# Duration table and operand margin of the clock that orders the matmuls, in a hybrid attention, gMLP and RWKV-7 layer

## The chip, the cores and the metric

The kernel runs on one core of a Trainium2 chip. The metric is the device time of one execution in microseconds (us). Five engines work side by side, each through its own instructions in program order: TensorE (PE in the profile, with its weight loads as PEld), VectorE (DVE), ScalarE (ACT), GpSimd (POOL) and SyncE (SP), which here issues almost all DMAs. An engine waits for another through semaphores. What stands early in an engine's program and is not ready holds back all that stands behind it on that engine.

## The reference

One layer with 2048 frames and 1024 channels, in float32. All branches read one projection of the normalised input, are gated, projected and merged:

```python
h = rmsnorm(x, pre_g[l]) * (1 + scale[:, None]) + shift[:, None]
q_lat, kv_lat, k_rope, gm_in, rw_in, z, g_logit = split_last(h @ w_in[l], IN_SPLITS)
y_mla = mla_mixer(...)      # 8 heads, softmax over chunk-causal keys
y_gm = gmlp_mixer(...)      # spatial gating inside blocks of 128 frames
y_rw, v_first = rwkv7_mixer(...)   # recurrence over all frames, a 64x64 state per head
branches = branches * jax.nn.silu(z)...
proj = jnp.einsum('bsnw,nwd->bsnd', branches, w_br[l])
merged = jnp.sum(proj * jax.nn.sigmoid(g_logit)..., axis=2)
x = x + gate[:, None] * rmsnorm(merged @ w_out[l], post_g[l])
```

## The kernel before

The sequence is cut into four blocks of 512 frames (`NSB` = 4). After a first stage that prepares block 0, each block s goes through two stages. `wkv(s)` is the RWKV branch: for four pairs of heads `project` and `prepare` make operands, `inverses` solves small triangular systems on VectorE in 31 dependent steps, `advance` makes the per-chunk matrices and `states` walks the eight chunks of the block one after the other (matmul `pss<-S,QG`, then two VectorE copies `S<-pss`, then the next chunk). `attention(s)` is the softmax branch: 8 heads with two units each; a unit computes scores (`pss<-kh,qh` and two more matmuls, since each float32 product is made of three matmuls on a high and a low part), takes minimum and exponential (`p`), transposes the result in groups of two key tiles (`pst<-consts,p`), splits it into `ph` (ScalarE copy) and `pw` (VectorE subtraction) and multiplies with the values (`pso<-ph,v`, `pso<-pw,v`). The last block ends with `finish`.

The large projections (`gemm`, matmuls into `pd`, 128x512 each, three per pair of operands) do not depend on these chains, and fill PE between their steps. Their weights come from DRAM, as raw weights that are split and stored the first time, and as stored parts (`kept`) afterwards.

No order of PE is written down. The program is generated by coroutines, and `Pace` keeps a clock while it is generated. Every emitted instruction passes through `Pace.note` (line 123 is the wrapper, which is why all profile rows say L123). `note` gives it a duration from small formulas by engine and size and places it in that engine's list of busy times, so each buffer has a time at which it is written or released. `Pace.run` then chooses which coroutine goes on: each yields the operands that it needs next, `ready` turns them into a time, and the one with the lowest time is stepped. Coroutines have ranks. The two chains of a stage (`behind`, `ahead`) and their helpers have ranks below 2. `todo` (rank 3, the next block's inputs) and `later` (rank 4, gates, branch projections, merges) hold the filler. Two rules tie filler to chains: a chain step that has to wait for an operand gets its time raised by `MARG` when it is compared, so filler that is ready is preferred unless the chain step is early by more than that; and in attention, filler is drawn as a share `SHARE[s]` of the chains' matmul time. The amount of filler in the whole program is fixed. The queue also supplies `backlog`, by which `split_lo` and `split` send the low part of new weights to VectorE or GpSimd.

The lines of the choice:

```python
r = k = self.ready(th)
if first and r > self.t:
    continue
if r > 0 and th[0] < 2:
    k += MARG
```

Of the kernel before, what the change touches and what calls it, by code (L numbers as in the profile page):

```python
# [36 lines left out]
DLAT = 0.8  # L37
EAR = 8.0
LAG = 1
MARG = 0.2  # L40
HOP = 0.25
SLOW = 1.0
KD = D // P
# [49 lines left out]
class Pace:  # L93
# [60 lines left out]
    def note(self, i):  # L154
        eng = str(i.engine).split(".")[-1]
        dma = "DMA" in type(i).__name__
        src, dst, n, full, f32 = [], [], 1, 0, False
        for l, aps in ((src, i.ins), (dst, i.outs)):
            for a in aps:
                ap = getattr(a, "bass_ap", None)  # L160
                if ap is None:
                    continue
                l.append(ap.tensor.name)
                m = 1
                for _, c in a.ap[1:]:
                    m *= c
                full += l is src and m > 1
                if dma:
                    m = 4 * m * a.ap[0][1]
                if eng != "PE" or l is dst:  # L170
                    n = max(n, m)
                elif a.dtype == F32:
                    f32 = True
        dep = 0.0
        for x in src:
            dep = max(dep, self.after(self.wrote.get(x), eng))
        for x in dst:
            for e in self.used.get(x, {}).items():
                dep = max(dep, self.after(e, eng))
        if eng == "PE":  # L180
            if f32 and not i.is_transpose:
                dur = 2 * max(.111, n * 2 / 2400)
            elif f32:
                dur = max(.108, n * 2 / 2400)
            else:
                dur = max(.061, n / 2400 + .0135)
            (r, c), (nr, nc) = i.tile_position, i.tile_size
            if dep <= self.t and all(r >= b or r + nr <= a for a, b in self.beside[1]):

                at = self.beside[0]  # L190
                self.beside[1].append((r, r + nr))
            else:
                at = max(self.t, dep)
                self.beside = at, [(r, r + nr)]
            t, p = max(self.t, at + dur), self.t
            self.pe += t - max(p, at)
            self.t = t
        elif dma:
            dur = n / 3.6e5
            t = self.slot("queue", max(dep, self.t - self.early), .45) + 1.1  # L200
            t = self.slot("DMA", t, dur) + dur + DLAT
            eng = "DMA"
        else:
            psum = any(x.startswith(("pd", "ps")) for x in src)
            op = type(i).__name__
            if eng == "Activation":
                f = str(i.func).split(".")[-1]
                if f in ("Exp", "Gelu", "Sin") and f != self.table or f == "Tanh" and self.table not in ("Exp", "Gelu"):
                    self.table = "Exp" if f == "Tanh" else f
                    t = self.slot(eng, max(dep, self.t - self.early), 1.28)  # L210
                dur = .08 + n * .00084 + .04 * (not psum) + .09 * (len(src) > 1) + .09 * (len(dst) > 1)
            elif eng == "DVE":
                dur = .065 + n / (960 if psum or full > 1 or n < 128 else 1920) + .065 * (full < len(src))
                if "Reciprocal" in op:
                    dur = .07 + n * .0063
                elif "Scan" in op or "Reduce" in op:
                    dur = n * (.0021 if "Scan" in op else .00118)
            else:
                dur = .12 + n * .00216 if n <= 512 else .55 + n * .0013
                if n <= 16 and "TensorTensor" in op:  # L220
                    dur = .3 + n * .165
            dur *= SLOW

            port = ("port",) if eng == "Pool" or eng == "DVE" and not psum else ()
            t = self.slot(eng, max(dep, self.t - self.early), dur, port) + dur
        for x in dst:
            self.wrote[x] = (eng, t)
        for x in src + dst:
            u = self.used.setdefault(x, {})
            u[eng] = max(u.get(eng, 0.0), t)  # L230
# [60 lines left out]
    def run(self, until, share=0.0, spare=lambda: True):  # L291
# [3 lines left out]
        while not until():  # L295
            best, key, at = None, self.INF, 0.0
            for first in ((3, 4, 0) if debt > 0 else (0,)):
                for th in self.threads:
# [5 lines left out]
                    if r > 0 and th[0] < 2:  # L304
                        k += MARG
                    if not first and th[0] == 4 and not spare():
# [1463 lines left out]
```

## Time and profile before

| | |
|---|---|
| time, median of 3 runs | 3148.54 us (3146.9 to 3155.53) |
| the profiled execution's own time | 3146.36 us |
| its span, first to last instruction | 3144.4 us |
| PE busy | 2927.0 us (93%) |
| DVE, ACT, POOL busy | 1731.6, 1216.7, 621.5 us |
| DMA | 654.17 MB, mean 208 GB/s |
| mean granted TensorE clock | 0.964 |

The span is one timeline of the core. An engine's busy share is an average over stages with different limits. The granted clock is the share of TensorE's full speed in a stretch: 1.0 is the higher of its two levels, 0.5 the lower, and a value between is a mix in time. A row of the view of windows gives, for one stretch, the busy time of each engine with the count of its instructions, the granted clock, the share of DMA engines in use and the rate. Stages lie at these times: first stage 0 to 236 us, `wkv(0)` 236 to 624, `attention(0)` from 624, then the stages of blocks 1 and 2, `wkv(3)` to 2712, `attention(3)` 2712 to 3027, `finish` to the end.

### The profile page before, as it was taken

Reading aid. Unit: us, or ns where it says so; the run is one execution under the profiler, and the core shown is the slowest. Engines: PE = TensorE matmul, PEld = TensorE weight load, DVE = VectorE, ACT = ScalarE, POOL = GpSimd, SP = SyncE. Lnnn points to the kernel's source line nnn. Section 1 sums busy time; section 2 is a strip of 40 time slices with the busy share of each in tenths; the row PEclk is TensorE's granted clock in tenths of the full one; section 3 lists DMA queues with packets and bytes.
Section 4 is the critical chain, followed back from the end, with each engine's and each line's share of the span. In section 5 each row is a group of like instructions: output and inputs, shape, how many; then the busy total and the mean of one; then the engine's idle time right before and its main releaser. Section 6 shows DMA issues by size and latency. Waiting matters only on the chain. (4 is left out here: it accounts for less than half of the span.)

```text
span 3144.4 us, 47954 instructions
## 1 busy us (share of the span) xinstructions
PE 2927.0 (93%) x16156; PEld 2391.6 (76%) x16156; DVE 1731.6 (55%) x4578; ACT 1216.7 (39%) x2806; POOL 621.5 (20%) x618
## 2 busy tenths in 40 slices
PE   5889998789999999999999998999999999999997
PEld 4667776668867787878877776887787777788876
DVE  6434767365366654466356664446645665566632
ACT  4324433353333424444232323544433232466621
POOL 2223232241022212122011101113201110222210
PEclk8999999879999999999999998999999999999998
DMA  8888855767566678765676577556558657744366
GB/s 273 271 271 264 251 182 182 242 210 229 200 210 223 192 226 265 225 196 166 211 251 199 166 230 231 185 177 209 155 169 250 198 171 230 224 137 128 113 207 204
DMA packets 524962, 654.17 MB, mean 208 GB/s; under 512 B 141648, under 2 KB 254380, under 8 KB 524716
## 3 DMA queue, kind: packets, MB, share of 16 engines
q1 hardware_dynamic: 524544, 651.06, 65.9%
q8 instruction: 128, 2.10, 0.3%
q14 instruction: 118, 0.97, 0.1%
q10 hardware_dynamic: 172, 0.05, 0.0%
HBM read 461.91 MB, written 189.01 MB: 207 GB/s over the span
## 5 line engine op out<-in xcount | busy, mean ns | idle before, releaser
L123 PE MATMUL pd<-hh,wh 128*128 128x512 f32 x1952 | 814.5, 417 | 19.3 <-ACT wh L123 10.3
L123 PE MATMUL pd<-hh,wl 128*128 128x512 f32 x1952 | 776.2, 398 | 6.1 <-DVE wl L123 4.3
L123 PE MATMUL pd<-hl,wh 128*128 128x512 f32 x1952 | 774.6, 397 | 2.5 <-DVE hl L123 1.5
L123 PEld LDWEIGHTS pd<-hh,wh 128*128 128x128 f32 x1952 | 374.5, 192 | 102.9 <-ACT wh L123 13.2
L123 PEld LDWEIGHTS pd<-hh,wl 128*128 128x128 f32 x1952 | 372.9, 191 | 94.7 <-DVE wl L123 8.3
L123 PEld LDWEIGHTS pd<-hl,wh 128*128 128x128 f32 x1952 | 374.8, 192 | 70.2 <-DVE hl L123 3.4
L123 DVE TENSOR_TENSOR pw<-pst,ph 128x512 fp32r<-128x512 f32 (+2 forms) x352 | 197.0, 568 | 255.2 <-ACT ph L123 253.6
L123 PE MATMUL pd<-brh,wh 128*128 128x512 f32 x576 | 252.0, 438 | 23.0 <-DVE gt L123 13.6
L123 ACT ACTIVATE ph<-pst 128x512 fp32r<-128x512 f32 (+2 forms) x352 | 171.7, 497 | 235.8 <-PE pst L123 197.8
L123 PE MATMUL pd<-brl,wh 128*128 128x512 f32 x576 | 232.4, 404 | 1.3 <-DVE brl L123 1.3
L123 PE MATMUL pd<-brh,wl 128*128 128x512 f32 x576 | 232.4, 403 | 0.0
L123 DVE TENSOR_SCALAR_CACHE_REDUCE p<-pss 128x512 f32<-128x512 f32 (+2 forms) x320 | 192.6, 607 | 62.6 <-PE pss L123 58.7
L123 ACT ACTIVATE p<-p,nm 128x512 f32<-128x512 f32 (+3 forms) x288 | 189.8, 661 | 79.1 <-DVE nm L123 78.9
L123 POOL TENSOR_TENSOR wl<-wr,wh 128x512 fp32r<-128x512 f32 x96 | 129.2, 1347 | 442.1 <-ACT wh L123 362.9
L123 ACT ACTIVATE wh<-wr 128x512 fp32r<-128x512 f32 x162 | 101.5, 628 | 220.0 <-PE pd L123 75.7
L123 PE MATMUL pst<-consts,p 128*128 128x128 f32 x1088 | 165.2, 277 | 7.9 <-DVE otm L123 3.1
L123 PEld LDWEIGHTS pd<-brh,wh 128*128 128x128 f32 x576 | 112.3, 195 | 58.6 <-DVE gt L123 11.6
L123 PE MATMUL pso<-ph,v 128*128 128x256 f32 x576 | 153.5, 287 | 2.4 <-ACT ph L123 2.3
L123 PE MATMUL pso<-pw,v 128*128 128x256 f32 x576 | 149.2, 286 | 6.3 <-DVE pw L123 6.0
L123 PEld LDWEIGHTS pst<-consts,p 128*128 128x128 f32 x1088 | 130.4, 143 | 24.7 <-issue 6.5
L123 PE MATMUL pss<-kh,qh 96*128 96x512 f32 (+2 forms) x320 | 131.1, 410 | 18.8 <-ACT kh L123 18.1
L123 POOL TENSOR_TENSOR kl<-stg,kh 96x512 fp32r<-96x512 f32 x80 | 103.8, 1300 | 223.8 <-ACT kh L123 194.6
(291 smaller groups left out, 4947.5 us busy)
## 6 DMA issues: line engine op xcount, KB each, us to landing
wh<-kept SPq DMA_DIRECT2D x486, 256.0 KB
wl<-kept SPq DMA_DIRECT2D x486, 256.0 KB
kept<-wh SPq DMA_DIRECT2D x162, 256.0 KB
kept<-wl SPq DMA_DIRECT2D x162, 256.0 KB
wr<-in_w_in SPq DMA_DIRECT2D x120, 256.0 KB
gate_d<-gt SPq DMA_DIRECT2D x64, 256.0 KB
part_d<-gt SPq DMA_DIRECT2D x64, 256.0 KB
p<-part_d SPq DMA_DIRECT2D x64, 256.0 KB
```

The source lines that it names most:

```text
L123: r = f(*a, **k)
```

## The change

Two kinds of numbers in `Pace` change; no instruction's own work is touched. `MARG` goes from 0.2 to 0.6 us. The fixed part of the durations goes up: for ScalarE from 0.08 to 0.165 us, for VectorE from 0.065 to 0.155, for GpSimd from 0.12 to 0.19 (short) and 0.55 to 0.6 (long), with the formulas for reductions and scans set anew.

```diff
-MARG = 0.2
+MARG = 0.6
@@ Pace.note
-                dur = .08 + n * .00084 + .04 * (not psum) + .09 * (len(src) > 1) + .09 * (len(dst) > 1)
+                dur = .165 + n * .00084 + .04 * (not psum) + .09 * (len(src) > 1) + .09 * (len(dst) > 1)
             elif eng == "DVE":
-                dur = .065 + n / (960 if psum or full > 1 or n < 128 else 1920) + .065 * (full < len(src))
+                dur = .155 + n / (960 if psum or full > 1 or n < 128 else 1920) + .065 * (full < len(src))
                 if "Reciprocal" in op:
                     dur = .07 + n * .0063
                 elif "Scan" in op or "Reduce" in op:
-                    dur = n * (.0021 if "Scan" in op else .00118)
+                    dur = .15 + n * (.0021 if "Scan" in op else .00105)
             else:
-                dur = .12 + n * .00216 if n <= 512 else .55 + n * .0013
+                dur = .19 + n * .00216 if n <= 512 else .6 + n * .0013
                 if n <= 16 and "TensorTensor" in op:
-                    dur = .3 + n * .165
+                    dur = .38 + n * .165
```

Through them the order of the program changes on every engine. PE executes the same matmuls in another order: the number of filler matmuls (`pd`) that stand between the first and the last score matmul of `attention(0)` to `attention(3)` goes from 372, 663, 843 and 405 to 420, 816, 864 and 96; between the last score of block 0 and the first of block 1, where `wkv(1)` lies, it goes from 1140 to 1368, and in the next two such stretches it is 1218 and 1152 before, 1212 and 1152 after. Between two chunk steps of `states` there stand mostly 6 filler matmuls before, and mostly 9 after.

The first place is the end of `wkv(0)` on PE. `Pm`, `u`, `n`, `MB`, `UV` are the steps of `advance`, `S,QG` the chunks of `states`, `Y` the output of the last pair of heads, and `kh,qh` the first scores of `attention(0)`. Before:

```order
L123 MATMUL pss<-S,QG 128x64 x2
L123 MATMUL pd<-hh,wh 128x512
L123 MATMUL pd<-hl,wh 128x512
L123 MATMUL pd<-hh,wl 128x512
L123 MATMUL pss<-S,QG 128x64 x6
L123 MATMUL pss<-consts,Y 128x128 x4
L123 MATMUL pss<-kh,qh 128x128
```

These are the last steps; ahead of them the last pair's chain has 48 more filler matmuls between its steps. With the change the same pair stands like this on PE:

```order
L123 MATMUL pd<-hh,wl 128x512
L123 MATMUL pss<-Pm,xtb 128x128 x8
L123 MATMUL pss<-u_5609,m_5544 128x128 x4
L123 MATMUL pss<-u_5616,m_5544 128x128 x4
L123 MATMUL pss<-n_5623,xtb 128x128 x4
L123 MATMUL pss<-n_5630,xtb 128x128 x4
L123 MATMUL pss<-MB,Wm 64x128 x16
L123 MATMUL pss<-UV,MB 128x64 x16
L123 MATMUL pss<-sst,QG 128x64 x2
L123 MATMUL pss<-S,QG 128x64 x14
L123 MATMUL pss<-consts,Y 128x128 x4
L123 MATMUL pss<-kh,qh 128x128
```

No filler is left inside it: the filler that a first block has stands earlier. The third pair's chain just ahead has none either, and between the two chains stand 24 filler matmuls.

The second place is a stretch of `attention(3)` on PE, one group of two key tiles to the next. Before:

```order
L123 MATMUL pst<-consts,p 128x128 x4
L123 MATMUL pss<-kh,qh 128x512
L123 MATMUL pss<-kl,qh 128x512
L123 MATMUL pss<-kh,ql 128x512
L123 MATMUL pd<-hh,wh 128x512
L123 MATMUL pd<-hl,wh 128x512
L123 MATMUL pd<-hh,wl 128x512
L123 MATMUL pso<-ph,v 128x256
L123 MATMUL pso<-pw,v 128x256
L123 MATMUL pso<-ph,v 128x256
L123 MATMUL pso<-pw,v 128x256
L123 MATMUL pst<-consts,p 128x128 x4
```

A triple of filler stands between the scores and the products with the values, in almost every group of the stage. With the change, at the same depth of the stage:

```order
L123 MATMUL pst<-consts,p 128x128 x4
L123 MATMUL pss<-kh,qh 128x512
L123 MATMUL pss<-kl,qh 128x512
L123 MATMUL pss<-kh,ql 128x512
L123 MATMUL pso<-ph,v 128x256
L123 MATMUL pso<-pw,v 128x256
L123 MATMUL pso<-ph,v 128x256
L123 MATMUL pso<-pw,v 128x256
L123 MATMUL pst<-consts,p 128x128 x4
```

The triple is gone, and so it is for 1233 matmuls in a row (7.2 of the 8 heads, at 172 matmuls a head), up to the end of the stage. The end of `attention(2)` has a stretch of 259 matmuls without filler, about 2 heads of that block; before it had none over 41. The last branch projection (`part` with n = 2), which stood behind `attention(3)` before, stands inside the stage after the change.

## Rows read from the trace of the kernel before

**Rows 1.** The page: span, and PE's busy time, share and instructions.
```profile
span 3144.4 us, 47954 instructions
PE 2927.0 (93%) x16156; PEld 2391.6 (76%) x16156; DVE 1731.6 (55%) x4578; ACT 1216.7 (39%) x2806; POOL 621.5 (20%) x618
```

**Rows 2.** Windows: stretch, length, busy time of each engine, PEclk, DMA share, GB/s.
```profile
0.00:236.00 236.00, 180.53 (x743) 138.62 (x744) 109.93 (x171) 81.57 (x145) 59.90 (x72) 0.92 0.84 272
236.00:624.00 388.00, 348.27 (x2022) 276.34 (x2020) 231.80 (x589) 146.75 (x283) 108.57 (x91) 0.96 0.72 224
624.00:2712.00 2088.00, 1993.57 (x11124) 1629.62 (x11124) 1164.10 (x3192) 764.84 (x1840) 361.99 (x366) 0.97 0.66 208
2712.00:3027.00 315.00, 310.68 (x1875) 272.61 (x1876) 192.83 (x577) 207.60 (x507) 75.94 (x73) 0.99 0.44 134
3027.00:3145.00 118.00, 93.95 (x395) 74.38 (x393) 32.96 (x50) 15.97 (x33) 15.05 (x19) 0.90 0.70 234
```

**Rows 3.** Waits of PE: total us, times, longest, whole span.
```profile
PE pss L123 <- ACT kh L123: 18.1, 4, 6.6
PE pd L123 <- DVE gt L123: 14.8, 10, 4.4
...
PE pss L123 <- DVE Y L123: 10.4, 5, 7.3
...
PE pso L123 <- DVE pw L123: 6.0, 7, 1.8
...
PE pss L123 <- POOL kl L123: 4.5, 4, 1.5
...
PE pss L123 <- DVE S L123: 2.7, 5, 0.8
```

**Rows 4.** Groups by form, window of `attention(3)` (2724 to 3015 us): count, busy, mean ns.
```profile
L123 ACT ACTIVATE p<-p,nm 128x512 f32<-128x512 f32 x104 | 74.2, 715 | 16.2 <-DVE nm L123 16.1
L123 ACT ACTIVATE ph<-pst 128x512 fp32r<-128x512 f32 x101 | 58.2, 591 | 39.9 <-PE pst L123 39.3
L123 ACT ACTIVATION_READ_ACCUMULATOR p<-p,nm 128x1 f32 x128 | 24.3, 190 | 0.0
...
L123 DVE TENSOR_TENSOR pw<-pst,ph 128x512 fp32r<-128x512 f32 x100 | 67.6, 689 | 63.6 <-ACT ph L123 63.4
...
L123 POOL TENSOR_TENSOR kl<-stg,kh 96x512 fp32r<-96x512 f32 x28 | 35.9, 1288 | 29.5 <-ACT kh L123 25.0 <-DMA stg<-kp_d 4.2
...
L123 PE MATMUL pd<-hh,wh 128*128 128x512 f32 x112 | 47.5, 424 | 0.0
...
L123 PE MATMUL pd<-brh,wh 128*128 128x512 f32 x32 | 13.1, 409 | 0.0
```

**Rows 5.** Chain that ended last: start us, us, a run of 27 filler matmuls.
```profile
2338.64 6.16 PE pd L123 x27
```

**Rows 6.** Timeline of PE: start us, us, instructions [idle before <-releaser]; chunk steps, end of `wkv(0)`.
```profile
452.19 4.67 PE L123 MATMUL pss<-S,QG 64*128 64x64 f32 x24 [0.67 <-DVE S L123]
...
599.87 0.44 PE L123 MATMUL pss<-S,QG 64*128 64x64 f32 x4
...
601.82 0.44 PE L123 MATMUL pss<-S,QG 64*128 64x64 f32 x4
...
616.54 1.09 PE L123 MATMUL pss<-consts,Y 128*128 128x128 f32 x4 [7.35 <-DVE Y L123]
624.21 0.47 PE L123 MATMUL pss<-kh,qh 96*128 96x128 f32 x1 [6.59 <-ACT kh L123]
```

**Rows 7.** Timeline of ACT and DVE: last inputs, first and last step of one `inverses`.
```profile
503.59 1.15 ACT L123 ACTIVATE abc<-pst 64x128 f32<-64x128 f32 x4 [0.46 <-PE pst L123]
...
513.08 0.25 DVE L123 SCALAR_TENSOR_TENSOR X<-mb,X 128x31 f32<-128x31 f32 x1 [1.33 <-DMA mb<-md]
...
546.94 0.17 DVE L123 TENSOR_TENSOR X<-X,tx 128x8 f32<-128x8 f32 x1
```

**Rows 8.** Windows, as rows 2: last two chains of `wkv(0)`, start of `attention(0)`, `attention(3)`.
```profile
520.00:567.00 47.00, 43.50 (x270) 35.04 (x269) 32.53 (x97) 13.38 (x24) 15.25 (x13) 1.00 0.67 211
580.00:617.00 37.00, 28.21 (x203) 23.08 (x202) 15.75 (x40) 10.37 (x19) 9.47 (x8) 0.90 0.70 230
624.00:660.00 36.00, 30.11 (x122) 26.07 (x123) 21.40 (x88) 25.86 (x77) 17.86 (x18) 0.58 0.66 180
2724.00:3015.00 291.00, 289.84 (x1772) 255.17 (x1770) 182.40 (x554) 198.27 (x490) 65.16 (x63) 1.00 0.44 131
```

**Rows 9.** Timeline of PE behind `attention(3)`, as rows 6.
```profile
3044.52 0.80 PE L123 MATMUL pd<-brh,wh 128*128 128x512 f32 x1 [4.37 <-DVE gt L123]
```

## The prediction

> **What bounds the kernel now.** I read the page first: PE is busy 93% of the span [rows 1]. The matmuls are the same before and after, so the time can only move by what is not matmul at full speed: idle time of PE, and stretches at the lower clock. The windows by stage show where that is [rows 2]; length less PE's busy time is its idle time. It is 55.5 us in the first stage, 39.7 in the first RWKV stage, 94.4 in the long middle from 624 to 2712 us, 4.3 in the last attention stage and 24.0 behind it. The last attention stage, with filler in nearly every group, has almost nothing to gain; the middle has 94.4 us spread over 2088.
>
> Then I read PE's waits, whose releaser tells whether a new order can help [rows 3]. The longest kind (18.1 and 4.5 us, ScalarE's and GpSimd's parts of the keys) is the fetch of a stage's first keys from DRAM, which is issued when the stage opens: a larger margin doesn't shorten it. The 14.8 us behind `gt` is filler that waits, for a bank or for data from DRAM, not a chain operand. What the change aims at is the rest: waits for `Y`, `pw`, `S` and some thirty kinds of 1 to 7 us. One row is a warning: all waits for a chunk's state `S` sum to 2.7 us.
>
> **The change part by part.** The sum is made against the profiled execution, 3146.4 us; the median of the runs shown is 2.2 us above it.
>
> *The durations.* They do what they say. For a 512-element subtraction from PSUM the old formula gives 0.065 + 512/960 = 0.60 us, the new one 0.69; the trace has 0.689. For ScalarE's copy it is 0.51, now 0.60, against 0.591; for GpSimd's subtraction 1.23, now 1.30, against 1.288 [rows 4]. So the clock sees an operand some 0.09 us later for each engine on its way, and the margin adds 0.4 us to every wait of a chain.
>
> *Waits in the middle.* Of 94.4 us idle I take off some 16 for the key fetches (22.6 less the 6.6 at 624 us) and some 8 for `gt`, which leaves 70 that a better order could reach. How much does it get? A filler matmul takes 6.16/27 = 0.228 us [rows 5]. Between two chunk steps there stood 6, or 1.37 us, and now 9, or 2.05. The step with 6 took 601.82 - 599.87 = 1.95 us without a wait; a bare one takes 4.67/6 = 0.78 [rows 6]. So 6 were enough there: the three more, seven steps in each of the sixteen chains at most, are up to 77 us of filler spent on a kind of wait worth 2.7 us. Filler is spent well only at the rarer steps. I take 40% of 70, **-28 us**; from -10 (the kinds of rows 3 one by one, a third of each) to -50 (nearly all that is reachable).
>
> *Clock in the middle.* Granted 0.97 over 2088 us [rows 2], that is 63 us below full speed if PE had work throughout. Dips follow waits, so a part goes with them: **-15 us**, from 0 to -30.
>
> *The first 520 us.* Idle there is 55.5 and, up to the last chain, about 27. But DMA is in use 0.84 at 272 GB/s, the highest of the five windows [rows 2]: the weights come and their parts go out. Filler drawn forward brings its weights forward too, on the same queue of SyncE and the same DMA engines. I take **-16 us**, from 0 to -30.
>
> *End of the first RWKV stage.* Filler of block 0 is a fixed amount, and it now runs out before the third pair's chain. The last pair's chain took 37.0 us with PE busy 28.2 [rows 8]; 51 filler matmuls in it are 11.6 us, so 25.4 are left, and what they hid has to be paid: 8 x 0.2 us at the chunk steps, some 2 at the matrices before them. A bare chain is thus 29 us with 16.6 of PE work, 12 us idle. The last pair had 8.8 us idle already (7.35 of it for `Y` [rows 6]): +3. The third pair had 3.5 us in 47 [rows 8]: +8.5. Between them the last pair's triangular systems must be done: 8.3 us from its inputs to the first step through DRAM and 34 more to the last [rows 7], on a VectorE that the chain shares, and the way back. Cover is a chain of 29, 24 fillers (5.5) and some 4 before: 38.5. With a freer VectorE I take a wait of 5, from 0 to 10. The bare end of `prepare` adds 3. That is 20. The clock adds to it: 0.90 in the last chain's window and 0.58 in the bare start of attention behind it [rows 8]. At 0.65, the bare 44 us of PE work would take 24 more; I take 13. Sum **+33 us**, from +12 to +60.
>
> *Bare attention.* In 291 us for eight heads PE was busy 289.8 [rows 8], of which 144 triples of filler (112 and 32 [rows 4]) are 98: 24.0 us a head of its own. ScalarE has 198.3 less about 12 for filler, 23.2 a head; VectorE about 21.5. Three engines nearly equal, in one loop: transposes, `ph` (0.591), `pw` (0.689), product with the values. That is 1.28 us from the transposes to the product even when both engines are free, and ScalarE also runs about one exponential (0.715 + 0.190) a group in between [rows 4]. PE has about 0.9 us of the neighbouring groups to put there, and 0.7 more where scores stand. The triple of filler was what closed that gap. I take 0.3 us of idle time a group, 15 groups: 4.6 a head, 28.6 in all. Over 7.2 bare heads that is 33, and 7 for the two smaller ones at the end of the stage of block 2. The lower bound is 0 (full overlap at 24.0 a head), the upper 0.74 a group, 11 a head, 95 in all. The clock may fall now and then: 8. Sum **+48 us**, from +10 to +95.
>
> *Last branch projection.* It moves from behind the last attention stage into it, and the wait of 4.37 us for its `gt` [rows 9] is covered: **-5 us**.
>
> The split of new weights between VectorE and GpSimd moves by seven (66 on VectorE, now 73) and costs nothing: neither engine is the bound in the stages where it happens. Shifts of single DMAs on SyncE's queue I cost at nothing as well; filler's weight fetches cover them while there is filler.
>
> Sum: -28 - 15 - 16 + 33 + 48 - 5 = **+17 us**, so 3163.4, and 3166 beside the median.
>
> **The rivals.**
>
> *Faster.* Attention needs no filler: its three engines overlap without it (+20 instead of +48, with single gaps only), and the first stage's bare end is short (+12). Then -28 - 15 - 16 + 12 + 20 - 5 = -32: 3117 us. For it speaks that most of a chain's steps were never waited for; against it that the equal load of three engines leaves no slack. It decides at a head time of about 26.5 us. Chance 0.28.
>
> *Much slower, by the clock.* Bare stretches run at the granted 0.58 of the only bare attention in the trace, 624 to 660 us [rows 8]. PE's 24.0 us a head become 41, so 17 a head more over 7.2 heads, 122 in place of 48: 3240 us. Against it: that stretch came after two waits of 7 us [rows 6], and its block has one key tile group where block 3 has four. Chance 0.10.
>
> The Trainium skill has this case: "TensorE: Matmul & The Clock Gate", section "A second HAM failure mode: psum-queue depth-cycling", says that a PE which idles briefly and often between matmul groups swings between its two clocks. No row of a bare stage of this block can confirm it here; if the rule held throughout, the rival's 3240 would be the time, and without it the 8 us of clock in my sum would be 0.
>
> *Nothing to measure.* The filler's gain and its absence cancel, within 0.3% (9 us, about what can be told from no change here): between 3139 and 3158 us. Chance 0.18. That the change does nothing is excluded by the order.
>
> **How the numbers follow.** My forecast, slower by the two bare stretches: 0.44 for times above 3158 and below 3225. With the clock rival, slower has 0.54, same 0.18, faster 0.28. The likeliest case gives 3166. The range reaches into the faster rival and to the upper bounds of the bare stretches, short of the full clock rival: 3105 to 3232.
>
> **What would show it.** Right: in the last attention stage PE is idle 30 us or more and heads take 27 to 31 us; at the end of the first RWKV stage PE waits 5 us or more for `xtb` or matrices of the third pair, with a granted clock near 0.6; in the middle PE's idle time is 55 to 75 us in place of 94. Wrong: a head time of 25 us at full clock, or idle time in the middle that doesn't fall (then the result is 3190 or more), or a first stage that ends much earlier than before.

## The result, and the profile after

The changed kernel takes 3266.14 us (median; 3263.63 to 3268.77) against 3152.03 us of the kernel before on the same chip: ratio 1.0363, 95% interval 1.0342 to 1.0384. The direction was forecast, the size was not: 114 us more than before, where +17 was predicted, and past the range's upper end of 3232.

The profiled execution took 3265.91 us. Page of the kernel after, answering to [rows 1]: span, and busy time, share and instructions of each engine.

```profile
span 3264.1 us, 47898 instructions
...
PE 2968.0 (91%) x16156; PEld 2416.1 (74%) x16156; DVE 1717.5 (53%) x4583; ACT 1226.7 (38%) x2814; POOL 606.4 (19%) x613
```

The span is 119.7 us longer. PE's busy time grew by 41.0 and its idle time by 78.7: with the same matmuls, the second is waiting. The first is for the most part the lower clock: the mean granted clock is 0.954 after and 0.964 before, which is worth at most 37 us (0.046 of 3264 us less 0.036 of 3144).

Windows of the kernel after by stage, as [rows 2] and [rows 8] (stretch, length, busy time of PE, PEld, DVE, ACT, POOL, granted clock, DMA share, GB/s). The first two are the first stage and `wkv(0)`, the third the middle, the fourth `attention(3)` from its first to its last score matmul, the fifth what lies behind it:

```profile
0.00:260.00 260.00, 202.01 (x841) 157.37 (x842) 112.86 (x169) 87.57 (x157) 60.58 (x75) 0.92 0.85 276
260.00:665.00 405.00, 343.36 (x1924) 274.25 (x1922) 227.81 (x595) 136.75 (x270) 97.72 (x83) 0.90 0.63 196
665.00:2909.00 2244.00, 2107.21 (x11568) 1717.06 (x11568) 1165.37 (x3210) 794.81 (x1873) 359.18 (x365) 0.97 0.65 205
2909.00:3153.00 244.00, 225.19 (x1377) 194.97 (x1378) 170.18 (x535) 178.97 (x455) 82.88 (x80) 0.96 0.35 99
3153.00:3265.00 112.00, 90.20 (x449) 72.48 (x447) 41.26 (x75) 28.56 (x63) 6.06 (x12) 0.95 0.51 169
```

The same cuts in the kernel before, behind the first score matmul at 624 us:

```profile
0.00:624.00 624.00, 528.80 (x2764) 414.96 (x2764) 341.73 (x760) 228.32 (x428) 168.48 (x162) 0.95 0.77 242
624.00:2713.00 2089.00, 1993.57 (x11124) 1629.62 (x11125) 1164.71 (x3193) 765.84 (x1842) 362.99 (x366) 0.97 0.66 208
2713.00:2997.00 284.00, 281.37 (x1688) 246.58 (x1689) 179.44 (x550) 193.65 (x477) 73.65 (x72) 0.99 0.45 134
2997.00:3145.00 148.00, 123.27 (x581) 100.40 (x580) 45.74 (x78) 28.92 (x61) 16.34 (x20) 0.92 0.64 213
```

Filler moves between these stretches, so lengths alone say little; each filler matmul that moves is taken off at its 0.228 us [rows 5]. All through this text the *excess* of a stretch is its length less that of before, less 0.228 us for each filler matmul that it has more. Up to the first score matmul both kernels do the same work: 665.5 less 624.2 us, **+41**. The middle has 444 matmuls more (11568 less 11124, all filler), 101 us, and is 155 us longer: **+54**. In `attention(3)` 309 filler matmuls are gone, 70 us, and it is 40 us shorter: **+31**. Behind it: **-6**. Of the middle's 54, 40 lie in its last two stages, `attention(2)` (+19) and `wkv(3)` (+21).

Waits of PE after, answering to [rows 3] (total us, times, longest):

```profile
PE pss L123 <- DVE Y L123: 25.1, 5, 7.7
PE pss L123 <- ACT kh L123: 21.0, 5, 7.6
PE pd L123 <- DVE gt L123: 19.6, 8, 5.7
PE pd L123 <- ACT brh L123: 13.8, 6, 4.6
PE pd L123 <- DVE wl L123: 13.5, 10, 2.7
...
PE pso L123 <- DVE ak L123: 12.7, 11, 4.7
PE pso L123 <- DVE pw L123: 12.1, 23, 2.4
...
PE pss L123 <- DMA xtb<-xd: 8.0, 1, 8.0
```

`Y` has grown from 10.4 to 25.1 us and `pw` from 6.0 to 12.1, the waits at which the change aimed. And PE waits longer in front of projection matmuls (`pd`), for filler's own inputs: over all of them 94.9 us, and 54.2 before. In the middle the chains' waits (into `pss`, `pso`, `pst`) sum to 82 us after and 80 before, those in front of `pd` to 54 and 20. The largest of those in front of `pd` in the middle, before (624.3 to 2713 us):

```profile
PE pd L123 <- DVE gt L123: 8.5, 6, 3.1
PE pd L123 <- ACT brh L123: 2.8, 1, 2.8
```

And after (665.6 to 2909 us):

```profile
PE pd L123 <- DVE gt L123: 15.6, 7, 5.7
PE pd L123 <- ACT brh L123: 13.8, 6, 4.6
PE pd L123 <- issue: 5.5, 3, 2.0
PE pd L123 <- ACT sq L123: 4.6, 1, 4.6
PE pd L123 <- DVE X L123: 4.5, 1, 4.5
```

Timeline of PE at the end of `wkv(0)` after, answering to [rows 6] (start, duration, instructions, idle before and its releaser):

```profile
608.89 1.09 PE L123 MATMUL pss<-consts,Y 128*128 128x128 f32 x4 [7.71 <-DVE Y L123]
...
624.62 3.75 PE L123 MATMUL pss<-Pm,xtb 128*128 128x128 f32 x16 [7.95 <-DMA xtb<-xd]
...
643.30 6.95 PE L123 MATMUL pss<-S,QG 64*128 64x64 f32 x28 [0.30 <-DVE S L123]
657.65 1.09 PE L123 MATMUL pss<-consts,Y 128*128 128x128 f32 x4 [7.40 <-DVE Y L123]
665.53 0.47 PE L123 MATMUL pss<-kh,qh 96*128 96x128 f32 x1 [6.79 <-ACT kh L123]
```

Four waits of 7 to 8 us where before had two: the third pair's `Y`, the last pair's inputs and its `Y`, and the keys.

### The profile page after: what moved, and what is told of

It is laid out like the page before. It is cut to its first block, busy times and chain, and to the rows that moved or that the text cites. A ratio compares the mean times of both kernels' runs of the same rounds, so it can differ in the third digit from the quotient of the medians.

```text
span 3264.1 us, 47898 instructions
## 1 busy us (share of the span) xinstructions
PE 2968.0 (91%) x16156; PEld 2416.1 (74%) x16156; DVE 1717.5 (53%) x4583; ACT 1226.7 (38%) x2814; POOL 606.4 (19%) x613
## 4 chain that ended last, share of the span: by engine, by line
PE 54%; DVE 9%; DMA 8%; issue 5%; ACT 4%; POOL 2%; SPq 1%; DVEq 0%; POOLq 0%; ACTq 0%
PE pd L123 33%; PE pss L123 10%; PE pst L123 8%; PE pso L123 3%; SPq L123 1%; DVE pw L123 1%; DVE X L123 1%; ACT p L123 1%; DVE p L123 1%; DMA stg<-kp_d 1%; DVE tx L123 1%; DMA mg_d<-gt 1%; ACT ph L123 1%; DMA x<-in_x 1%; DMA gt<-gate_d 1%
## 5 line engine op out<-in xcount | busy, mean ns | idle before, releaser
L123 PE MATMUL pd<-hh,wh 128*128 128x512 f32 x1952 | 806.0, 413 | 27.1 <-ACT wh L123 7.8
L123 PE MATMUL pd<-hh,wl 128*128 128x512 f32 x1952 | 774.4, 397 | 16.2 <-DVE wl L123 13.5
L123 POOL TENSOR_TENSOR wl<-wr,wh 128x512 fp32r<-128x512 f32 x89 | 119.3, 1342 | 418.0 <-ACT wh L123 322.5
L123 PE MATMUL pso<-ph,v 128*128 128x256 f32 x576 | 161.4, 300 | 4.6 <-ACT ph L123 4.6
L123 PE MATMUL pso<-pw,v 128*128 128x256 f32 x576 | 153.4, 293 | 12.7 <-DVE pw L123 12.1
L123 ACT ACTIVATE gt<-pd 128x512 f32<-128x512 f32 x96 | 56.9, 593 | 263.7 <-PE pd L123 252.1
```

What stands on the lines that cost most here:

```text
L123: r = f(*a, **k)
```

## The experiments

Each group of kernels was timed beside the kernel before anew, whose median was then 3150.32 to 3152.79 us; each ratio is against its own. An excess comes from one profiled execution. Where only a stage is changed, `pace.stage` counts the stages (0 the first, 1 `wkv(0)`, 2 `attention(0)`, up to 8 `attention(3)`).

**One half of the program at a time.** The new numbers only before `attention(0)`, and only from there on:

```diff
+                new = self.stage < 2        # later_blocks: self.stage >= 2
-                dur = .08 + n * .00084 + ...
+                dur = (.165 if new else .08) + n * .00084 + ...
...
-                        k += MARG
+                        k += .6 if self.stage < 2 else MARG
```

> The new durations and the new margin hold only up to the end of the first RWKV stage, the old ones from there on. The order of PE is that of the changed kernel up to the first attention stage and that of the kernel before behind it. If the cost of the change adds up stage by stage (filler that runs out where a chain still needs it), this costs what the traces show between the start and the first scores: 665.5 - 624.2 = 41 us, so about 3190 us. Rival: what is lost by then is won back, since the work is the same and later transfers start no later: within 10 us of before. If the cost came from DMA traffic over the whole program it would also be far under 41.

3192.36 us, ratio 1.0122 [1.0103, 1.0140].

> The reverse: old durations and margin up to the end of the first RWKV stage, new ones behind it. The order of PE is that of the kernel before up to the first attention stage, and that of the changed kernel from there. If costs add up stage by stage, 120 - 41 = 79 us more than before, about 3227 us. If the first block set the pace for all, within 20 us of before.

3227.06 us, ratio 1.0244 [1.0220, 1.0269]. The excess is +39 up to the first score and +8 behind it in the one, with no stage above 4; nothing and then +78 in the other, 53 of it in the middle. The losses of the stages add up, and the middle loses on its own, with no bare first stage ahead of it.

**Margin alone, durations alone.** `margin_only` changes `MARG` to 0.6 and nothing else, `durations_only` is the rest of the diff.

> Margin 0.6, old durations. Filler inside the last attention stage is 240 matmuls (405 before, 96 with the whole change), with 785 matmuls in a row without filler at its end (1233 with the whole change), and the last pair of the first RWKV stage has none inside its chain, the third pair has. If the margin is what spends the filler too early and the price is that of the bare stretches: about half of the changed kernel's 114 us, 40 to 70. If a larger margin removes waits elsewhere, as it is meant to, near before (within 15 us).

3180.24 us, ratio 1.0094 [1.0075, 1.0114].

> New durations, margin 0.2 as before. Filler inside the last attention stage is 267 matmuls, with 800 in a row without filler at its end; the last pair of the first RWKV stage has none inside its chain. If bare stretches set the price, as much as with the margin alone, 40 to 70 us, since the bare stretches are equally long. If a clock that is nearer to the trace makes a better order wherever there is filler, less than with the margin alone by 20 us or more.

3192.79 us, ratio 1.0127 [1.0108, 1.0145]. 28 and 41 us, and 114 together, so 45 come only of the two at once. The margin's 28 is below the 40 to 70 of the one theory and above the 15 of the other. The durations lose 48 in the first stage and `wkv(0)` and 11 in `attention(3)` and win 11 in the middle; the margin loses in several places, `attention(3)` (+14) the largest. Neither alone empties the last stage as the two do (240 and 267 filler matmuls stay there, 96 with both).

**Bare attention by itself.** The order of before, with rank 4 barred from `attention(3)`:

```diff
-                    if first and th[0] != first:
+                    if first and th[0] != first or self.stage == 8 and th[0] == 4:
                         continue
```

> The kernel before, with its filler (rank 4) barred from the last attention stage; the stage's 405 filler matmuls run behind it, all else stands as before. This prices bare attention by itself. In the changed kernel the last attention stage, 7.2 heads of it bare, took 30.9 us more than its filler explains, 4.3 us a head. If that is the price of bareness, eight heads cost 34 us and the time is about 3185. If attention by itself overlaps well and the changed kernel's loss there came from elsewhere (keys that arrive late, a low clock after a wait), under 15 us.

3202.04 us, ratio 1.0155 [1.0138, 1.0172]. Window of `attention(3)` in this run, from 5 us behind the first score matmul to the last:

```profile
2718.00:2935.00 217.00, 201.32 (x1275) 172.74 (x1275) 164.98 (x526) 175.24 (x450) 67.72 (x67) 0.97 0.21 55
```

The time is past the 3185 expected. In the stage itself (222 us) the excess is 30.6 us for eight heads, 3.8 a head, near the 4.3 expected; 9 us came in `wkv(3)` ahead of it and 14 behind, where the barred filler had to go.

**Holding filler back in the first stage.** `first_block`, with the rule that makes rank 4 dearer raised there:

```diff
-                        k = max(k, self.t) + LONG
+                        k = max(k, self.t) + (6.0 if self.stage == 0 else LONG)
```

> Like first_block (new durations and margin up to the end of the first RWKV stage, old behind it), but in the first stage the gate and branch filler is held back by 6 us in place of 1.5, so that it is left for the RWKV stage; the last pairs' chains have filler again. If the 40 us of first_block are the filler that was spent too early, most of it comes back: 3152 to 3165 us. If they come from the order inside the RWKV stage or from the new durations as such, it stays at 3190.

3171.23 us, ratio 1.0060 [1.0043, 1.0077]. A miss: half of the 40 us came back, not nearly all. Up to the first score the excess is 20 us with PE idle only 7 us more than before, but with a granted clock below full speed for 112 us where before has 66.

**Where the durations could help.** New durations in `attention(0)` to `attention(2)` alone, margin 0.2 (the diff of `first_block` with `self.stage in (2, 4, 6)` and without the last line):

> The kernel before with the new durations in the attention stages of blocks 0 to 2 alone, margin 0.2 everywhere. In durations_only those three stages took 10.1, 2.1 and 10.9 us less than before beside their filler, while the first block and the last attention lost. If the stages' costs add up here too, about 20 us less than before: 3132 us. If those gains were filler borrowed from the bare stages, which must be paid elsewhere, within 8 us of before.

3156.38 us, ratio 1.0013 [0.9985, 1.0042]. A miss: in the profiled execution, which is 6 us above the median, two stretches gained 7 and 8 us and two others lost 14 and 15. That filler given at one place was taken from another fits this, but isn't shown by it.

**Is it filler that waits for DRAM?** `later_blocks`, with the clock's DMAs 2.2 us longer there:

```diff
-            t = self.slot("DMA", t, dur) + dur + DLAT
+            t = self.slot("DMA", t, dur) + dur + (3.0 if self.stage >= 2 else DLAT)
```

> later_blocks (old constants up to the end of the first RWKV stage, new ones behind it) with one more change there: the clock puts 3.0 us in place of 0.8 on the landing of a DMA. The last attention stage is as bare as in later_blocks (96 filler matmuls). In later_blocks PE stands before projection matmuls, the filler's own, for 51 us between the first scores of block 0 and those of block 3, against 20 in the kernel before. If that is filler that is let ahead of chains while its data is still on the way from DRAM, a clock that knows of later landings takes 20 us or more of it away: 3200 us or less. If it is the chains' order or banks, it stays within 10 us of 3227.

3292.71 us, ratio 1.0425 [1.0385, 1.0465]: 66 us worse than `later_blocks`, where a gain was expected. PE's idle time in front of the middle's projection matmuls fell from 52 to 45 us alone, and the middle's excess rose from 53 to 131. So the theory that filler was drawn before its weights had come was not borne out. It isn't excluded either: the longer landing holds for the chains' own DMAs too, and the clock then plans 656 us of idle time for PE where it planned 421. A fourth duration made longer did the same as the three.

**The clock's own account.** That miss turned the question round: not which duration is wrong, but what all of them stand beside. The clock can be read out while the order is written. Its times are no measurement; the idle time of PE that it plans can be laid beside the trace's:

```
PE idle, us             to first score  middle  attention(3)  behind   sum
before, planned              142          75          4         14     234
before, traced                95          95          3         24     217
after, planned               221         181         77         20     499
after, traced                120         136         19         21     296
```

The clock of before lets PE work 2711 us (it ends at 2945, less the 234 idle); the trace has 2927.0 [rows 1]. That of after has 2713 against 2968.0. So it is 7.4 and 8.6% short (the expectation of `after_pe_scaled` says 2706), and the other engines were short too in the clock of before [rows 4]. The change brought three engines to the trace and left the fourth. In the new clock the chains' operands come late against a PE that is too fast; it plans twice the idle time, of which the trace shows a fraction (19 of 77 us in `attention(3)`). The reading that the next runs test is that it spends filler on waits that don't come.

**PE's own durations.** One line in `note`, ahead of the placing of a matmul:

```diff
+            dur *= 1.08
             (r, c), (nr, nc) = i.tile_position, i.tile_size
```

In the kernel after; in the kernel after with `MARG` 0.2; in the kernel before. And a fourth kernel, after with the margin on filler that isn't ready:

```diff
                     if r > 0 and th[0] < 2:
                         k += MARG
+                    elif r > 0:
+                        k += MARG
```

> The kernel after, with one line more: the clock's own durations of matmuls are multiplied by 1.08. In the clock of both kernels PE is busy 2706 us, in the traces 2927, so the change brought three engines to the trace and left the fourth 8% short. Theory (proportion): the clock of after therefore plans PE waits that don't exist: read out while the order is written, it plans 499 us of PE idle time, against 234 in the clock of before, and fills them with filler that is missing later. With PE scaled it plans 351. Then the first stage's +41 us falls to about +15 and the middle's +53 to about +25; the last attention stage keeps only 126 filler matmuls and its +25 to +30. Time about 3215. Rival (the margin and the longer chains themselves, whatever PE's scale): the extra filler in the first RWKV stage and the middle's waits stay, 3250 to 3270.

3171.26 us, ratio 1.0073 [1.0049, 1.0097]. Windows, with the cuts used above:

```profile
0.00:634.00 634.00, 540.42 (x2764) 423.44 (x2764) 337.66 (x753) 230.28 (x430) 171.70 (x169) 0.92 0.75 238
634.00:2810.00 2176.00, 2078.90 (x11539) 1700.96 (x11539) 1175.37 (x3207) 793.52 (x1870) 363.72 (x365) 0.98 0.67 210
2810.00:3049.00 239.00, 224.56 (x1411) 195.29 (x1411) 172.96 (x540) 181.54 (x460) 83.05 (x79) 0.99 0.38 111
3049.00:3162.00 113.00, 92.58 (x446) 74.34 (x445) 40.61 (x74) 27.83 (x62) 6.07 (x12) 0.93 0.50 168
```

95 of the 114 us are gone, twice as much as was expected (3215). Up to the first score +10 is left of +41; the middle has 415 matmuls more than before, 95 us, and is 87 us longer: -8 where after had +54. `attention(3)` keeps +19, since it is nearly as bare.

> The new durations, matmuls multiplied by 1.08 as well, and the margin back at 0.2: all four engines of the clock near the trace. Durations alone gave 3192.8. Theory (proportion): the clock plans 280 us of PE idle time in place of the 411 of durations alone, and 441 filler matmuls stay in the last attention stage, where 267 stood: 3150 to 3170. Rival (the longer chains themselves): the first stage still costs 40 us more than before, and the time is 3185 to 3195.

3138.96 us, ratio 0.9960 [0.9944, 0.9976]: 54 us below the durations alone, more than expected, and 0.4% faster than before.

> The kernel before with matmuls multiplied by 1.08 in the clock and nothing else: the opposite step, since now PE is at the trace and the other engines are short. The clock plans 177 us of PE idle time in place of 234 and spends less filler: 1494 matmuls before the first attention stage in place of 1560, 432 and 447 in the last attention stage and behind it in place of 405 and 423. Theory (proportion, and before already near its best): chains get barer, PE waits behind operands that the clock takes for ready; real waits of the chains grow by 20 to 40 us in the RWKV stages, while the end gains nothing: 3160 to 3180. Rival (filler is overspent in before already, so holding more of it back helps): 3130 to 3145, a version that beats both.

3136.46 us, ratio 0.9963 [0.9948, 0.9978]. Here the theory of proportion failed (3160 to 3180) and the rival was right: with PE alone at the trace and the other engines short, the kernel before gets faster too (-13 up to the first score, with 1494 filler matmuls there in place of 1560).

> The kernel after, with the margin of 0.6 us added to filler that isn't ready too, as to a chain's operand that isn't. In after PE is idle 94.9 us in front of filler and projection matmuls (54.2 before), and the clock planned 94.6 of it: filler that will be ready sooner than an operand plus 0.6 us is taken, and PE waits for it. Theory (PE waits for filler by the clock's own choice): that idle time falls by 15 to 20 us, to about 77, as the clock plans, and the time by 15 to 30, to 3235 to 3250. Rival (filler's supply, its weights and splits, is what is late): the idle time in front of these matmuls stays at 90 or more, and the time within 10 us of 3266.

3238.52 us, ratio 1.0291 [1.0265, 1.0317]. Some of its waits of PE in front of `pd`:

```profile
PE pd L123 <- DVE gt L123: 20.5, 9, 4.7
...
PE pd L123 <- ACT brh L123: 8.8, 5, 2.5
PE pd L123 <- DVE wl L123: 8.7, 6, 3.3
```

`brh` and `wl` are 8.8 and 8.7 us, 13.8 and 13.5 in after; all idle time in front of `pd` is 76.3, 94.9 in after, and the time is 28 us less. So part of PE's waiting for filler is the order's choice: filler that will be ready within 0.6 us of a chain operand goes first, and PE waits for it.

**Which proportion.** Scaling PE also shortens the clock's DMAs, hops between engines and margin beside it. `after_engines_092` leaves PE and sets `SLOW`, the factor on the three engines, to 0.92 in the kernel after; `before_all_108` takes the 1.08 on matmuls and `SLOW` = 1.08 in the kernel before; `durations_pe_115` is `durations_pe_scaled` with 1.15.

> The kernel after, with VectorE's, ScalarE's and GpSimd's durations in the clock multiplied by 0.92 and matmuls left alone: the three engines stand to PE as in the run with PE scaled by 1.08, while DMAs stand to PE as in after. Theory (proportion of engines to PE): most of the gain of that run, 3171 against 3266, is here too: 3165 to 3195. Rival (PE's scale helped because the clock's DMAs got shorter beside PE): the time stays at 3230 to 3266. The clock itself plans 387 us of PE idle time, 499 in after and 351 with PE scaled; by that count alone it would be 3195 to 3200.

3218.60 us, ratio 1.0186 [1.0162, 1.0211]. Outside both: 48 of the 95 us.

> The kernel before, with matmuls and the three engines all multiplied by 1.08 in the clock: the proportion of engines to PE is that of before, and only DMAs and the hop between engines are shorter beside them. Theory (proportion of engines to PE): 3142 to 3156, within 0.3% of before, though matmuls alone by 1.08 gave 3136. Rival (the clock's total against its DMAs is what the scale of PE changes): 3130 to 3140, as with matmuls alone.

3147.54 us, ratio 0.9976 [0.9959, 0.9994]. Inside the first theory's bounds, though a gain of a quarter per cent can be told from none.

> The new durations, margin 0.2 and matmuls multiplied by 1.15 in the clock: the same step as the run with 1.08, once more. The clock plans 217 us of PE idle time (280 with 1.08, 411 with 1.00), spends less filler in the middle and keeps 402 and 417 filler matmuls for the last attention stage and behind it. Theory (proportion, with its best place near the traces' 1.08): the chains get barer than they should and the time turns up again, 3140 to 3160. Rival (the less filler is planned for early, the better): 3115 to 3132.

3131.03 us, ratio 0.9913 [0.9891, 0.9936], the fastest of all. Its windows:

```profile
0.00:616.00 616.00, 530.58 (x2764) 414.15 (x2764) 336.77 (x752) 230.82 (x430) 176.40 (x170) 0.95 0.76 242
616.00:2701.00 2085.00, 1990.55 (x11133) 1625.98 (x11133) 1160.20 (x3195) 769.82 (x1843) 366.79 (x367) 0.97 0.67 210
2701.00:2990.00 289.00, 285.74 (x1702) 249.79 (x1703) 180.32 (x548) 192.78 (x478) 73.88 (x72) 0.98 0.44 129
2990.00:3133.00 143.00, 117.45 (x560) 95.52 (x558) 44.33 (x74) 27.60 (x59) 16.34 (x20) 0.95 0.66 217
```

The gain doesn't turn at the trace's own scale: with 9 matmuls more than before the middle is 4 us shorter, and the first part 8. The expectation that 1.08 is the best place fell.

All kernels by the idle time that their clock plans (PE idle, then median time, us):

```
                      planned  traced   time
before_pe_scaled        177      211    3136.46
durations_pe_115        217      208    3131.03
before_all_108          225      213    3147.54
before                  234      217    3150.39
attention_durations     241      229    3156.38
first_block_held        268      228    3171.23
durations_pe_scaled     280      219    3138.96
margin_only             297      231    3180.24
first_block             312      247    3192.36
bare_att3               331      251    3202.04
after_pe_scaled         351      225    3171.26
after_engines_092       387      258    3218.60
durations_only          411      248    3192.79
later_blocks            421      265    3227.06
after_filler_margin     471      270    3238.52
after                   499      296    3266.14
later_dram_known        656      295    3292.71
```

The order is not strict, and what is planned late in the program is a consequence as much as a cause (a last stage that has run out of filler is planned idle). But the six kernels that plan above 380 us are among the seven slowest, and of those that plan below 290 only `first_block_held` is clearly slower than before. How far times scatter between orders that differ by chance wasn't measured, so the gains of 0.2 to 0.9% on the kernel before (5 to 22 us) may in part be luck of an order; the differences of 50 us and more stand well above them.

## Why the prediction was wrong

*The durations.* That the new numbers are nearer the trace was right for each engine [rows 4], and I took "nearer" for "better" without looking at the fourth engine. The clock's sum for PE, 2711 against 2927 us, was to be had from the same kernel and the same page. In total the new clock is even the truer one: it ends at 3212 us against a span of 3264, that of before at 2945 against 3144. It gives the worse order.

*Waits in the middle, -28.* **This step failed.** I took 40% of 70 us of chain waits as reachable, because filler would stand in front of the rare long ones. The chains' waits stayed (80 and 82 us), and waits in front of filler came on top (20 to 54 us), so PE's idle time in the middle rose from 95 to 136 us where 55 to 75 were forecast; this was one of the prediction's own signs of being wrong. The step's own reading was the warning: six filler matmuls between two chunk steps were already enough, and nine were spent on a kind of wait worth 2.7 us. What was missing was the consequence: the filler isn't only wasted, it can be gone at the next place. The clearest case lies in `wkv(2)` after. Timeline of PE, last chunk steps of a pair:

```profile
1826.51 0.44 PE L123 MATMUL pss<-S,QG 64*128 64x64 f32 x4
...
1832.55 0.44 PE L123 MATMUL pss<-S,QG 64*128 64x64 f32 x4
1832.91 0.50 PE L123 MATMUL pd<-brh,wh 128*128 128x512 f32 x1
1833.25 0.39 PE L123 MATMUL pd<-brl,wh 128*128 128x512 f32 x1
1833.48 0.40 PE L123 MATMUL pd<-brh,wl 128*128 128x512 f32 x1
1841.54 1.08 PE L123 MATMUL pss<-consts,Y 128*128 128x128 f32 x4 [7.66 <-DVE Y L123]
```

24 filler matmuls stand between the two steps, which wait for nothing, and 3 ahead of `Y`, which comes 7.66 us late.

*Clock in the middle, -15.* Wrong with it: no waits went, the granted clock stayed at 0.97, and the middle's PE work took 12 us more than the 101 of its additional filler.

*First 520 us, -16, and the end of the first RWKV stage, +33.* Together +17, measured +41. The first stage has 624 filler matmuls in 260 us, 523 in 236 before; the 101 more are 23 of the 24 us. So it saved about nothing, inside the 0 to -30 given. From there to the first score there are 102 filler matmuls less, and it is 17 us longer: +40, inside +12 to +60. The waits were sized well: the last pair's inputs through DRAM were late by 7.95 us (5 were taken), the third pair's chain was idle 9.8 us where it had 3.5 (8.5 more were taken), and the last pair's `Y` waited 7.40 and 7.35 before (3 more were taken). In all, PE's idle time there rose by 22 us (20 taken) and its work, less filler, by 18 (13 taken for the clock, on 44 us of bare work where there were 54). Windows of the bare stretch after, as [rows 2]:

```profile
577.00:588.00 11.00, 9.13 (x90) 7.95 (x90) 6.66 (x15) 2.19 (x8) 2.49 (x2) 1.00 0.51 142
589.00:601.00 12.00, 11.70 (x51) 11.15 (x50) 7.31 (x39) 1.25 (x2) 0.00 (x0) 0.50 0.00 0
577.00:665.50 88.50, 54.39 (x322) 48.17 (x322) 45.70 (x142) 13.94 (x31) 10.32 (x10) 0.64 0.23 70
```

The 0.64 is the 0.65 of the prediction. But "dips follow waits" isn't the whole of it: the clock fell in the third pair's chain, between 588 and 589 us, with PE busy 9.1 of the 11 us ahead of that and 11.7 of the 12 behind, and that chain's one long wait still to come.

*Bare attention, +48.* Right in size at `attention(3)`: 4.3 us a head over 7.2 heads, where 4.6 were taken; `bare_att3` gives 3.8 over eight. The make-up was half right: PE's idle time there rose by 16 us, 4 of them in one wait in front of filler (the next point), so the groups' own is about 0.11 us each and not 0.3. The other half is PE itself, busy for 225.2 us where the 281.4 of before less 309 filler matmuls make 210.9. The lower clock, held for 21 us of the stage, is at most 10 of these 14; what the rest is stays open, and no row stood behind the 8 us that the sum had for the clock. The two smaller heads at the end of `attention(2)`, 7 us in the sum, belong to a stretch with an excess of 19.

*Last branch projection, -5.* Measured -6 behind `attention(3)`, but the mechanism was wrong and the number luck: the wait for `gt` wasn't covered, it moved into the stage with the projection and is part of the +31 there. Timeline of PE after:

```profile
2935.61 0.50 PE L123 MATMUL pd<-brh,wh 128*128 128x512 f32 x1 [4.05 <-DVE gt L123]
```

*The rival by the clock* was wrong for the stage that it named. The granted clock in the bare `attention(3)` is 0.96 (fourth window of after) and 0.97 in `bare_att3`, with PE at the lower level for 21 of 244 us. The excess of 31 us stands against the 122 of that rival. The Trainium skill, "TensorE: Matmul & The Clock Gate", section "A second HAM failure mode: psum-queue depth-cycling", describes a kernel whose PE idles briefly between groups of matmuls so often that it swings between its two clocks. This stage, with its 0.11 us of idle time a group, shows hardly any of that.

*The sum.* Of the 103 us between +17 and +120, 90 are the middle (-36 with the two heads of `attention(2)`, +54 measured), 24 the part up to the first score, and -11 the rest.

What stays open: why the engines' scale gives back only half of what PE's scale does. The other half must lie in what PE's scale shortens besides, DMAs, hops, the margin and the clock's other fixed times; these weren't tried apart, and on the kernel before the same relative step (`before_all_108`) is worth 0.24%. So for the proportion of the engines to PE half of the cause is shown. Nor is it known where the gain of a larger PE scale turns.

## What to carry to other kernels

A table of costs that sets an order is not better because more of its rows are right: bringing three engines to the trace and leaving the fourth short was worse here than leaving all four short. So sum the table's time for each engine over the whole program and lay it beside the busy row of the profile before any single row is corrected. Truth of the proportions is no guarantee either: PE alone at the trace beat the kernel before, and a PE made longer than its trace gave the fastest kernel. The idle time that the table plans, laid beside the trace's, told more about the order than the single rows did. Where filler is a fixed amount, a planned wait that doesn't exist can cost twice, since the same filler may be missing at a real one; count filler at both ends before crediting a gain. A margin that chain operands get and filler doesn't also makes the engine wait for filler that isn't ready.

## What the runs showed of the hardware

The granted clock doesn't fall in waits alone. In the third pair's bare chain it was 1.00 from 577 to 588 us and 0.50 from 589 to 601, where PE was busy 11.70 of 12 us with `pss<-UV,MB` and `pss<-S,QG`; the chain's long wait, 7.71 us up to the `Y` matmul at 608.89, had yet to come. That and three more waits of about 7 to 8 us followed within 57 us, and the clock was 0.64 from 577 us to the first score. So idle time doesn't measure the clock's cost: up to the first score PE is idle 95 us before and 120 after, 25 more, but at the lower clock for 66 and 121 us, 55 more; with filler held back in the first stage it was idle 7 us more and at the lower clock 46 us more. A bare `attention(3)`, with 19 us of idle time in 244, one wait of 4 us and the rest in pieces of about 1 us or less, kept a granted clock of 0.96. What sets the two stretches apart isn't shown by these runs.
